# The relative bias of the second mixer: joined in SBUF by accumulating transfers, or by additions on GpSimd

## The chip, the cores and the metric

The kernel runs on one core of one Trainium2 chip. The metric is device time in microseconds (us), taken over whole executions; the time before is the median of three runs. Engines carry the names of the profile: PE is TensorE, PEld its weight load, DVE VectorE, ACT ScalarE, POOL GpSimd, SP SyncE.

## The reference

Two blocks of two layers each run over 256 tokens of 1024 channels. The first block has latent attention, a squared-relu MLP, block attention with a relative bias, and another MLP; the second has a gated delta rule and a forgetting attention. The change concerns the bias of the block attention. With 256 tokens there is one block, so nothing is selected, and what is left is causal attention with eight heads of 128 channels:

```python
def rel_bias(pq, pk):
    return table_h[h_i4, t5_bucket(pq - pk)].astype(jnp.float32)
...
lg_own = (jnp.einsum('bhqd,bhtd->bhqt', qi, k_own).astype(jnp.float32) * scale
          + rel_bias(pq4, pos_own[:, None, None, :]))
causal = (own * MOBA_BLOCK + t_ids)[None, :] <= q_idx[:, None]
parts.append(jnp.where(causal, lg_own, -jnp.inf))
```

`t5_bucket` turns the distance of a query and a key into one of 32 buckets, and `table_h` has a number for each head and bucket.

## The kernel before

All matrix products of weights are made of three products of rounded parts. `load_w` (L148) brings 512 KB of weights into one of four buffers `raw` over SyncE's queue (L161), ScalarE rounds them to `whi` (L164), VectorE, or GpSimd where the call says so, subtracts to get `wlo` (L165), and `mm3` issues the products (L171 to L173). A buffer `raw` is free for the next load when its `wlo` is done. The instructions are written in one program order, layer by layer; a planner puts them on the engines' queues by when their inputs should be there, so an instruction may stand far ahead of its place in the program if it waits for nothing. Each engine then takes its queue strictly in order.

The bias is made during the first MLP, which runs 16 steps `f` of 256 hidden channels. Each step loads two pieces of `mlp_w_in` and two of `mlp_w_out`. `rel_bias_step` (L379) hangs on each step: VectorE makes masks that say which keys each bucket reaches (L377), TensorE multiplies them by the differences of the table (L393), and ScalarE copies the result to a staging buffer (L395), of which there are two. The table is in two parts, a rounded one and the rest, so there are two partial sums, `part` 0 and 1. After every second step `b`, eight transfers of 64 KB on GpSimd's queue send the staging buffer to `bias_d` in DRAM (L400); `bias_d` is [part, query, head, key].

After the MLP `rel_bias_finish` (L403) reads it back so that queries lie on partitions. Two transfers bring part 0 into `bias` (L404, L405), four bring part 1 into two buffers `b2` (L409, L410), and for each half of the heads GpSimd adds the two parts (L411) and the causal mask (L412): four additions of 128 x 1536 numbers. `bias` is [128, 8 heads, 384]: the first 128 columns are the first 128 queries against the first 128 keys, the other 256 the second 128 queries against all keys. It lies in `bias_s`, beside the positions `pk` and `pq` from which the masks are made. `attend` (L312) adds it to the logits, first at L321.

The second mixer `moba` (L720) follows. It transposes x (L256, L257, L271), takes the mean square and its inverse root (`ms_eps`, `rsqrt` with L182 to L187, VectorE's work on 128 x 2 numbers), and projects queries, keys and values (`qkv_quad`, L682) before the first head is attended to.

The program at its end is `mla()`, `rel_bias_setup()`, `mlp(0, ...)` with the bias step, `rel_bias_finish()`, `moba()`, `mlp(1)`, `gdn()`, `fox()`. `rel_bias_setup` makes `pk`, `pq` and the table's differences, and clears their tile `tw` (L367).

Of the kernel before, what the change touches and what calls it, by code (L numbers as in the profile page):

```python
# [19 lines left out]
P = 128  # L20
# [4 lines left out]
H = 8  # L25
# [17 lines left out]
# smallest distance of each of the 32 relative-position buckets; the first takes every distance below 1  # L43
# [15 lines left out]
def layout(inputs):  # L59
    """The small operands side by side as [128, n]: constants, gains with one channel on each  # L60
    partition, rows that every partition needs; and where each begins and ends."""
# [10 lines left out]
    # causal mask for [query tile 0 x keys 0..127 | query tile 1 x keys 0..255]  # L72
# [23 lines left out]
    # identity columns of the 32 x 32 blocks that the partitions (column half, block, unit) solve for  # L96
# [14 lines left out]
def kernel(ctx: ExitStack, tc: tile.TileContext, I: dict, out: bass.AP, small_at: dict):  # L111
# [11 lines left out]
    # ------------------------------------------------------------------ helpers  # L123
    def slot(i, shape, dt=F32):
        """one of the 8 KB (8: 16 KB) places that the stages share"""
        return big.tile(shape, dt, tag=f"s{i}", name=f"s{i}")
# [13 lines left out]
    @contextmanager  # L140
    def queued(after):
        """what the block issues comes behind the instructions given, each on its engine"""
        with ExitStack() as es:
            for i in after or ():
                es.enter_context(tc.issue_after(i))
            yield

    def load_w(src, a, b, engines=None, into=None, after=None):  # L148
        """DRAM [128, a, b] -> for each i < a the two float32r parts, [128, b] each"""
        m = max(1, 1024 // b)  # L150
        parts = []
        for a0 in range(0, a, m):
            k = min(m, a - a0)
            raw = ring.tile([P, 1024], F32, tag="raw", name="raw")
            if into is None:
                hi = ring.tile([P, 1024], F32R, tag="whi", name="whi")
                lo = ring.tile([P, 1024], F32R, tag="wlo", name="wlo")
            else:
                hi, lo = (t[:, a0 * b:(a0 + k) * b] for t in into)
            rs = raw[:, :k * b]  # L160
            nc.sync.dma_start(rs.rearrange("p (a b) -> p a b", a=k), src[:, a0:a0 + k])  # L161
            e = V if engines is None else engines[a0 // m % len(engines)]
            with queued(after):
                A.activation(hi[:, :k * b], rs, AF.Copy)  # L164
                e.tensor_tensor(lo[:, :k * b], rs, hi[:, :k * b].bitcast(F32), op=ALU.subtract)  # L165
            for i in range(k):
                parts.append((hi[:, i * b:(i + 1) * b], lo[:, i * b:(i + 1) * b]))
        return parts
# [9 lines left out]
    def rsqrt(dst, x, n):  # L178
        """dst = x ** -0.5 for [128, n] tiles"""
# [9 lines left out]
    def rsqrt_sum(r, e, a, b):  # L189
        """r = ((a + b) / D + eps) ** -0.5 for [128, 1] tiles; e [128, 2] is room; D = 4 ** 5"""  # L190
# [9 lines left out]
    # ------------------------------------------------------------------ inputs and constants  # L200
# [18 lines left out]
    # keep the tensor engine's clock up until the first weights are here  # L219
# [4 lines left out]
    # per-channel scales that carry the attention scale too  # L224
# [7 lines left out]
    # ------------------------------------------------------------------ shared stages  # L232
    def mean_sq(dst, src_t, t):
        """dst [128, 2]: sums of squares of the two halves of a token tile"""
        for hf in range(2):
            j = w2k([P, 512])
            A.activation(j, src_t[:, t, hf * 512:(hf + 1) * 512], AF.Square, accum_out=dst[:, t, hf:hf + 1])

    def ms_eps(src, name, after=None):
        """[128, 2]: mean square over the row, plus eps"""  # L240
# [9 lines left out]
    def evac_split(hi, lo, p, g=None):  # L250
        """PSUM p (times a per-partition gain) into two float32r parts"""
# [11 lines left out]
    def transpose_x(src, gnames, slots):  # L263
        """src token-major [128, 2, 1024] -> for each gain the split transposed [128, 8, 256]"""
# [17 lines left out]
    def proj_tok(hT, w, c0, n):  # L282
        """token-major product of hT (1024 rows) and columns c0..c0+n (n <= 512): two accumulators"""
# [10 lines left out]
    def out_proj(oT, w, then, between=None):  # L294
        """oT [128, 8, 256] times w [1024, 1024] by column halves; then(t, half, psum)"""
# [16 lines left out]
    def attend(logits, scale, bias, v, oT, h):  # L312
        """one head: logits(ps) fills [128, 384]; scale: None or [128, 1] per query tile; v [128, 2, 128]"""
# [36 lines left out]
    # ------------------------------------------------------------------ relative bias for the second mixer  # L350
    bias = bias_s[:, 0:3072].rearrange("p (h k) -> p h k", h=H)
    bias_d = dr.tile([2, S, H, S], F32, tag="bias_d", name="bias_d")

# [20 lines left out]
    def masks(i, pq, pk):  # L374
        """which keys each of the 32 buckets reaches, for four groups of queries"""
# [3 lines left out]
    def rel_bias_step(i, pq, pk, tw):  # L379
        """four of the 64 groups; every eighth group sends what there is to DRAM"""  # L380
# [15 lines left out]
        if half == 1:  # L396
            for part in range(2):
                for q4 in range(4):
                    r0 = part * 32 + q4 * 8
                    nc.gpsimd.dma_start(  # L400
                        bias_d[part, 64 * q4 + 8 * b:64 * q4 + 8 * b + 8].rearrange("g h k -> h g k"), stg[r0:r0 + 8])

    def rel_bias_finish():  # L403
        nc.gpsimd.dma_start(bias[:, :, 0:128], bias_d[0, 0:128, :, 0:128])  # L404
        nc.gpsimd.dma_start(bias[:, :, 128:384], bias_d[0, 128:256])  # L405
        for h4 in range(2):
            hs = slice(4 * h4, 4 * h4 + 4)
            b2 = slot(13 + h4, [P, 4, 384])
            nc.gpsimd.dma_start(b2[:, :, 0:128], bias_d[1, 0:128, hs, 0:128])  # L409
            nc.gpsimd.dma_start(b2[:, :, 128:384], bias_d[1, 128:256, hs])  # L410
            G.tensor_tensor(bias[:, hs], bias[:, hs], b2, op=ALU.add)  # L411
            G.tensor_tensor(bias[:, hs], bias[:, hs], cmask[:, None, :].to_broadcast([P, 4, 384]), op=ALU.add)  # L412

    # ------------------------------------------------------------------ layer 0: latent attention
    def rope_tables():
# [7 lines left out]
        # quarter turn for the cosine enters with the turn count, so that the reduction stays exact  # L423
# [29 lines left out]
    def rope_apply(eng, dst, src, tab, nh):  # L453
        """src, dst [128, 2, nh, 64]; tab: the cosine and the sine table with the gain in them"""
# [8 lines left out]
    def mla():  # L463
# [65 lines left out]
        # eps terms of the per-head norms: the rows still carry the scale of the norms before  # L529
# [84 lines left out]
    # ------------------------------------------------------------------ squared-relu MLP  # L614
    def mlp(l, extra=None):
# [16 lines left out]
        for f in range(NF):  # L632
            wc = load_w(w1[:, :, f * 256:(f + 1) * 256], KD, 256, (G,) if f == 0 else None, after=last if f == 1 else None)
            r = w2k([P, 512])
            if f == 0:
                # the upper half of the rows comes last out of the stage before
# [38 lines left out]
    # ------------------------------------------------------------------ layer 1: block attention with relative bias  # L675
    def head_sumsq(dst, src):
        """dst [128, 4]: sums of squares of four heads of src [128, 512]"""
# [4 lines left out]
    def qkv_quad(hTq, hTk, wq, cq, wkk, ck, wv, cv, es, g4, gq, gk, qT, kT, vt, vscale, a=None):  # L682
        """four heads: q transposed (its norm is left to the logits: rq), k normed and transposed, v"""
# [57 lines left out]
    # ------------------------------------------------------------------ norms of the second block  # L741
    def row_scale(r, rb):
        """r [128, 2] with the tokens along the free axis, on every partition"""
# [5 lines left out]
    def post_norm_out(oT, w, gname, after, between=None):  # L749
        """x += rms_norm(oT.T @ w) * gain; after(t) once a token tile is done"""  # L750
# [20 lines left out]
    def softplus_neg(dst, u_in, n):  # L771
        """dst = log(1 + exp(-u_in)) for u_in >= 0, by the series of the inverse hyperbolic tangent"""
# [18 lines left out]
    # ------------------------------------------------------------------ gated delta rule  # L791
    def gdn():
# [7 lines left out]
        # gates  # L800
# [30 lines left out]
        # running sums of the log decays in each chunk, as columns and as rows  # L831
# [30 lines left out]
        def conv(part, dst, hp):  # L862
            """two heads: product, causal depthwise convolution over time, silu; channels on partitions"""
# [20 lines left out]
        def token_sumsq(dst, p, hp):  # L884
            """sums of squares of two heads of tokens, p [128, (t, head, channel)]"""
# [6 lines left out]
        # keys: their products within a chunk, and the diagonal blocks of the triangular system  # L892
# [32 lines left out]
        # inverses of the 32 x 32 diagonal blocks: partition (half of the columns, block, unit)  # L925
# [12 lines left out]
        def substitute(j):  # L938
            """row j of the inverse is done: take its part out of the rows below"""
# [59 lines left out]
        def gate(q4):  # L999
            """the gate of four heads, with the gain of the output norm in it"""  # L1000
# [6 lines left out]
        def grow_a(s, u4):  # L1007
            """block inverses from s to 2 s; X[:, 0] the inverse, X[:, 1] its transpose"""
# [46 lines left out]
        # chunk 0, the state it leaves, chunk 1  # L1055
# [28 lines left out]
        def solve(t, q4):  # L1084
            """what the chunk adds to the state, on the scale of the keys as they are"""
# [48 lines left out]
    # ------------------------------------------------------------------ forgetting attention  # L1134
    def fox():
# [3 lines left out]
        # the first token tile goes ahead while the second one is still being normed  # L1139
# [64 lines left out]
        def gates():  # L1204
            # the row scale along the free axis
# [31 lines left out]
    # ------------------------------------------------------------------ program  # L1237
    mla()
    rb = rel_bias_setup()
    mlp(0, lambda f: rel_bias_step(f, *rb))  # L1240
    rel_bias_finish()
# [28 lines left out]
```

## Time and profile before

| | us |
|---|---|
| median of three runs | 1002.09 |
| lowest, highest run | 1000.29, 1003.99 |
| span of the profiled execution | 996.2 |

The profile gives the profiled execution's time as its span, from the first to the last instruction; it has no other time for it, and the runs' times, taken around a whole execution, are some 6 us longer. Times in a row count from the span's start. A row of a timeline has the start, the duration, the engine, the line, the operation, what it writes and reads, and in brackets how long the engine had been idle and what ended that. [...]

### The profile page before, as it was taken

Reading aid. Unit: us, or ns where it says so; the run is one execution under the profiler, and the core shown is the slowest. Engines: PE = TensorE matmul, PEld = TensorE weight load, DVE = VectorE, ACT = ScalarE, POOL = GpSimd, SP = SyncE. Lnnn points to the kernel's source line nnn. Section 1 sums busy time; section 2 is a strip of 40 time slices with the busy share of each in tenths; the row PEclk is TensorE's granted clock in tenths of the full one; section 3 lists DMA queues with packets and bytes.
Section 4 is the critical chain, followed back from the end, with each engine's and each line's share of the span. In section 5 each row is a group of like instructions: output and inputs, shape, how many; then the busy total and the mean of one; then the engine's idle time right before and its main releaser. Section 6 shows DMA issues by size and latency. Waiting matters only on the chain.

```text
span 996.2 us, 14682 instructions
## 1 busy us (share of the span) xinstructions
PE 913.5 (92%) x5462; PEld 792.4 (80%) x5462; DVE 673.7 (68%) x1323; ACT 516.1 (52%) x954; POOL 202.5 (20%) x217
## 2 busy tenths in 40 slices
PE   9699889999999889999999999878879897999996
PEld 8576579999997677778999999668877785789874
DVE  6897476556555875766545554669996588767766
ACT  7574354645454545656544444357634224856653
POOL 1320121111122700022000002243496403000000
PEclk9899799999999989999999999979999999999998
DMA  8343237666667555435665666334646204365431
GB/s 294 104 148 106 64 117 230 203 191 191 193 196 242 173 169 166 141 110 191 207 206 174 188 197 180 93 86 127 159 128 179 76 22 132 103 217 184 132 123 64
DMA packets 96552, 154.61 MB, mean 155 GB/s; under 512 B 9160, under 2 KB 60128, under 8 KB 96224
## 3 DMA queue, kind: packets, MB, share of 16 engines
q1 hardware_dynamic: 91168, 141.53, 45.9%
q0 software_dynamic: 5168, 12.10, 4.4%
q8 instruction: 43, 0.70, 0.3%
q14 instruction: 29, 0.24, 0.1%
q10 hardware_dynamic: 144, 0.03, 0.0%
HBM read 147.84 MB, written 5.78 MB: 154 GB/s over the span
## 4 chain that ended last, share of the span: by engine, by line
PE 51%; DVE 17%; DMA 13%; ACT 8%; issue 5%; POOL 5%; SPq 0%; DVEq 0%; ACTq 0%; POOLq 0%
PE acc L171 11%; PE acc L172 10%; PE acc L173 10%; DMA raw<-in_mlp_w_in_dram 7%; DVE wlo L165 4%; ACT whi L164 3%; PE aux L173 3%; PE aux L171 3%; PE aux L172 3%; POOL s L943 2%; POOL s L941 2%; DVE s L165 2%; DVE rs_b L185 1%; PE aux L1026 1%; PE aux L335 1%
## 5 line engine op out<-in xcount | busy, mean ns | idle before, releaser
L165 DVE TENSOR_TENSOR wlo<-raw,whi 128x1024 fp32r<-128x1024 f32 (+2 forms) x182 | 225.5, 1244 | 185.1 <-ACT whi L164 172.7
L164 ACT ACTIVATE whi<-raw 128x1024 fp32r<-128x1024 f32 (+3 forms) x206 | 210.6, 1025 | 228.3 <-DMA raw<-in_mlp_w_in_dram 131.9
L172 PE MATMUL acc<-wlo,s 128*128 128x512 f32 (+2 forms) x424 | 167.6, 396 | 8.6 <-DVE wlo L165 8.3
L171 PE MATMUL acc<-whi,s 128*128 128x512 f32 (+2 forms) x424 | 169.8, 405 | 4.6 <-ACT whi L164 2.9
L173 PE MATMUL acc<-whi,s 128*128 128x512 f32 (+2 forms) x424 | 166.5, 396 | 0.0
L173 PE MATMUL aux<-s,wlo 128*128 128x256 f32 (+2 forms) x528 | 150.2, 284 | 3.0 <-DVE wlo L165 3.0
L171 PE MATMUL aux<-s,whi 128*128 128x256 f32 (+2 forms) x528 | 150.2, 285 | 2.1 <-DVE s L257 2.1
L172 PE MATMUL aux<-s,whi 128*128 128x256 f32 (+2 forms) x528 | 149.9, 284 | 0.0
L165 POOL TENSOR_TENSOR wlo<-raw,whi 128x1024 fp32r<-128x1024 f32 (+2 forms) x24 | 55.2, 2316 | 241.3 <-ACT whi L164 240.5
L171 PEld LDWEIGHTS aux<-s,whi 128*128 128x128 f32 (+2 forms) x528 | 99.8, 189 | 4.6 <-DVE s L257 2.6
L173 PEld LDWEIGHTS aux<-s,wlo 128*128 128x128 f32 (+2 forms) x528 | 99.8, 189 | 4.4 <-DVE wlo L165 3.4
L171 PE MATMUL acc<-s,w2k 128*128 128x512 f32 x256 | 100.1, 391 | 2.4 <-ACT w2k L656 2.4
L172 PEld LDWEIGHTS acc<-wlo,s 128*128 128x128 f32 x424 | 81.9, 193 | 24.8 <-DVE wlo L165 11.2
L172 PEld LDWEIGHTS aux<-s,whi 128*128 128x128 f32 (+2 forms) x528 | 99.9, 189 | 1.9
L171 PEld LDWEIGHTS acc<-whi,s 128*128 128x128 f32 x424 | 81.1, 192 | 24.9 <-ACT whi L164 4.4
L173 PE MATMUL acc<-s,w2k 128*128 128x512 f32 x256 | 100.2, 392 | 0.1
L172 PE MATMUL acc<-s,w2k 128*128 128x512 f32 x256 | 100.1, 391 | 0.0
L173 PEld LDWEIGHTS acc<-whi,s 128*128 128x128 f32 x424 | 81.5, 192 | 15.5 <-DVE s L254 0.6
L165 DVE TENSOR_TENSOR s<-raw,s 128x1024 fp32r<-128x1024 f32 x60 | 70.8, 1220 | 4.8 <-ACT s L164 4.8
L172 PE MATMUL acc<-s,whi 128*128 128x256 f32 x256 | 73.6, 288 | 0.0
L171 PE MATMUL acc<-s,whi 128*128 128x256 f32 x256 | 73.5, 287 | 0.0
L173 PE MATMUL acc<-s,wlo 128*128 128x256 f32 x256 | 73.4, 287 | 0.0
(351 smaller groups left out, 1569.8 us busy)
## 6 DMA issues: line engine op xcount, KB each, us to landing
raw<-in_mlp_w_in_dram SPq DMA_DIRECT2D x64, 512.0 KB, 5.0
raw<-in_mlp_w_out_dram SPq DMA_DIRECT2D x64, 512.0 KB, 3.9
raw<-in_gdn_w_in_dram SPq DMA_DIRECT2D x32, 512.0 KB, 4.0
raw<-in_moba_w_qkv_dram SPq DMA_DIRECT2D x24, 512.0 KB, 4.1
raw<-in_fox_w_in_dram SPq DMA_DIRECT2D x16, 512.0 KB, 4.8
raw<-in_kv_w_dram SPq DMA_DIRECT2D x16, 512.0 KB, 4.0
raw<-in_mla_w_o_dram SPq DMA_DIRECT2D x8, 512.0 KB, 3.9
bias_d<-s POOLq DMA_DIRECT2D x64, 64.0 KB, 4.3
```

Source lines behind the costliest of these rows:

```text
L164: A.activation(hi[:, :k * b], rs, AF.Copy)
L165: e.tensor_tensor(lo[:, :k * b], rs, hi[:, :k * b].bitcast(F32), op=ALU.subtract)
L171: T.matmul(o, lhsT=l[0], rhs=r[0], start=start, stop=False)
L172: T.matmul(o, lhsT=l[0], rhs=r[1], start=False, stop=False)
L173: T.matmul(o, lhsT=l[1], rhs=r[0], start=False, stop=stop)
L185: V.scalar_tensor_tensor(b, dst, -0.5, x, op0=ALU.mult, op1=ALU.mult)
L335: T.transpose(pt[:, j * P:(j + 1) * P], pr[:, j * P:(j + 1) * P], ident)
L941: G.tensor_tensor(t3[:, 0:n, 0:c], xb[:, j, 0:c][:, None, :].to_broadcast([P, n, c]), bt[:, j, j + 1:32][:, :, None].to_broadcast([P, n, c ...
L943: G.tensor_tensor(xb[:, j + 1:32, 0:c], xb[:, j + 1:32, 0:c], t3[:, 0:n, 0:c], op=ALU.subtract)
L1026: T.matmul(px[z][:, j * P:(j + 1) * P], lhsT=a, rhs=b, start=True, stop=True)
```

## The change

Before the first MLP a new function writes the causal mask into `bias`, once for each head, by one transfer from the input `small` in DRAM on GpSimd's queue. `rel_bias_finish` goes, with its six loads, its buffers `b2` and its four additions. In its place a gather follows every second set of stores (after b = 1, 3, 5 and 7): for both parts and four groups of 64 queries, a transfer of 16 queries from `bias_d` that adds to what lies in `bias`. A transfer writes 16 partitions, 8 heads and 128 or 256 columns. The rest of the diff takes out comments and texts of functions, which changes no instruction.

```diff
+    def rel_bias_mask():
+
+        nc.gpsimd.dma_start(bias, I["small"][:, None, small_at["cmask"][0]:small_at["cmask"][1]].to_broadcast([P, H, 384]))
...
                     nc.gpsimd.dma_start(
                         bias_d[part, 64 * q4 + 8 * b:64 * q4 + 8 * b + 8].rearrange("g h k -> h g k"), stg[r0:r0 + 8])
-
-    def rel_bias_finish():
-        nc.gpsimd.dma_start(bias[:, :, 0:128], bias_d[0, 0:128, :, 0:128])
-        nc.gpsimd.dma_start(bias[:, :, 128:384], bias_d[0, 128:256])
-        for h4 in range(2):
-            hs = slice(4 * h4, 4 * h4 + 4)
-            b2 = slot(13 + h4, [P, 4, 384])
-            nc.gpsimd.dma_start(b2[:, :, 0:128], bias_d[1, 0:128, hs, 0:128])
-            nc.gpsimd.dma_start(b2[:, :, 128:384], bias_d[1, 128:256, hs])
-            G.tensor_tensor(bias[:, hs], bias[:, hs], b2, op=ALU.add)
-            G.tensor_tensor(bias[:, hs], bias[:, hs], cmask[:, None, :].to_broadcast([P, 4, 384]), op=ALU.add)
-
+            if b % 2:
+                rel_bias_gather(b - 1)
+
+    def rel_bias_gather(b):
+
+        for part in range(2):
+            for q4 in range(4):
+                p0, r = 64 * (q4 % 2) + 8 * b, 64 * q4 + 8 * b
+                a0, n = ((0, 128), (128, 256))[q4 // 2]
+                nc.gpsimd.dma_start(bias[p0:p0 + 16, :, a0:a0 + n], bias_d[part, r:r + 16, :, 0:n], accum_op=ALU.add)
...
     mla()
+    rel_bias_mask()
     rb = rel_bias_setup()
     mlp(0, lambda f: rel_bias_step(f, *rb))
-    rel_bias_finish()
     moba()
```

## Rows read from the trace of the kernel before

**Rows 1.** The page, busy time, share and instructions of each engine.

```profile
PE 913.5 (92%) x5462; PEld 792.4 (80%) x5462; DVE 673.7 (68%) x1323; ACT 516.1 (52%) x954; POOL 202.5 (20%) x217
```

**Rows 2.** Waits from 320 to 352 us: in total, times, longest.

```profile
PE acc L172 <- DVE wlo L165: 7.6, 1, 7.6
...
POOL s L411 <- DMA s<-bias_d: 5.6, 1, 5.6
```

**Rows 3.** Chain of waits, 318 to 352 us: start, duration, what.

```profile
334.69 4.47 DVE wlo L165
...
350.31 1.15 DVE wlo L165
```

**Rows 4.** Timeline of GpSimd: the first and the last of four additions.

```profile
334.58 3.50 POOL L411 TENSOR_TENSOR s<-s,s 128x1536 f32<-128x1536 f32 x1 [5.59 <-DMA s<-bias_d]
...
346.01 3.42 POOL L412 TENSOR_TENSOR s<-s,small 128x1536 f32<-128x1536 f32 x1
```

**Rows 5.** Timeline of VectorE in the same stretch.

```profile
333.40 1.23 DVE L165 TENSOR_TENSOR wlo<-raw,whi 128x1024 fp32r<-128x1024 f32 x1
...
346.19 3.27 DVE L185 SCALAR_TENSOR_TENSOR rs_b<-r,mse 128x2 f32<-128x2 f32 x1
349.49 0.16 DVE L186 TENSOR_TENSOR rs_b<-rs_b,r 128x2 f32<-128x2 f32 x1
```

**Rows 6.** Timeline of TensorE around its gap.

```profile
343.52 0.39 PE L171 MATMUL acc<-whi,s 128*128 128x512 f32 x1
351.50 0.80 PE L172 MATMUL acc<-wlo,s 128*128 128x512 f32 x1 [7.59 <-DVE wlo L165]
...
355.42 0.39 PE L172 MATMUL acc<-wlo,s 128*128 128x512 f32 x1
```

**Rows 7.** Windows: length, then busy (count) by engine, clock, DMA share, GB/s.

```profile
351.50:355.40 3.90, 3.90 (x9) 3.11 (x10) 3.90 (x4) 0.00 (x0) 0.00 (x0) 0.51 0.71 201
```

**Rows 8.** Timeline of ScalarE: the rounding behind the late `wlo`.

```profile
338.78 1.05 ACT L164 ACTIVATE whi<-raw 128x1024 fp32r<-128x1024 f32 x1
```

**Rows 9.** Timeline of GpSimd at the start.

```profile
0.88 0.20 POOL L367 MEMSET tw<- 128x128 f32 x1
```

**Rows 10.** Windows: the first loads, and the quiet stretch before the first MLP.

```profile
4.00:20.00 16.00, 14.74 (x84) 13.82 (x83) 12.17 (x40) 12.79 (x23) 1.83 (x2) 1.00 0.98 350
...
120.00:135.00 15.00, 12.91 (x69) 10.66 (x69) 8.27 (x19) 5.90 (x15) 0.00 (x0) 0.89 0.00 1
```

**Rows 11.** Chain of waits, 0 to 26 us.

```profile
9.25 7.96 DMA x<-in_x_dram
```

**Rows 12.** The page, DMA queues: packets, MB, share of 16 engines.

```profile
q0 software_dynamic: 5168, 12.10, 4.4%
```

**Rows 13.** Chain of waits, 150 to 560 us: loads inside the first MLP.

```profile
204.62 6.57 DMA raw<-in_mlp_w_in_dram
...
217.76 4.62 DMA raw<-in_mlp_w_in_dram
...
228.93 5.52 DMA raw<-in_mlp_w_in_dram
...
289.69 4.68 DMA raw<-in_mlp_w_in_dram
...
300.92 6.16 DMA raw<-in_moba_w_qkv_dram
```

**Rows 14.** Timeline of GpSimd: two of the eight sets of stores.

```profile
225.26 4.44 POOL L400 DMA_DIRECT2D bias_d<-s  x8 [19.88 <-ACT s L395]
248.53 4.44 POOL L400 DMA_DIRECT2D bias_d<-s  x8 [18.83 <-ACT s L395]
```

**Rows 15.** Instructions on `bias_d`: issue in ns, first and last start; landing.

```profile
L400 POOL DMA_DIRECT2D bias_d<-s x64: 562/562/842, 151.3 to 322.3; - x64
...
DMA to landing us min/median/max: 3.0/4.4/8.5
```

**Rows 16.** Instructions of line 321, `attend`: ns, first and last start.

```profile
L321 DVE SCALAR_TENSOR_TENSOR w2k<-aux,r,s x32: 341/412/480, 379.3 to 978.1; 128x128 f32<-128x128 f32 x16, 128x256 f32<-128x256 f32 x16
```

## The prediction

> **What bounds the kernel now.** The page comes first. TensorE is busy 92% of the span [rows 1], so an edit on GpSimd or on the DMA queues gains only where TensorE stands still, and costs only where it makes TensorE stand. I then read the waits around the edited code, between the first MLP and the second mixer. There the longest wait of TensorE is 7.6 us for a `wlo` of VectorE [rows 2]. The chain of waits passes the same place: from 334.69 to 350.31 it runs over VectorE alone, and its first step is a `wlo` of 4.47 us [rows 3]. The reader is to see that this is no long work: the same `wlo` took 1.23 us just before, and a 128x2 step that takes 0.16 us a little later takes 3.27 us here [rows 5]. What else was going on is in GpSimd's timeline: four additions of 128x1536, back to back, from 334.58 to 349.43 [rows 4]. The stretched steps of VectorE end where these end. So I read it as one engine keeping the other out: VectorE does four stretched steps in the time of four additions, and the `wlo` that TensorE needs waits behind them.
>
> TensorE's timeline gives the price. A matmul starts at 343.52, the next at 351.50, and the usual pace is back at 355.42 [rows 6]. The gap is about 7.75 us. [...] In all **9.6 us**.
>
> **The change part by part.**
>
> *Four additions leave GpSimd.* VectorE is then free from 334.6. The `whi` that the waiting `wlo` needs is started at 338.78 and takes 1.05 us [rows 8], so with 1.23 us the `wlo` is ready at about 341.1, before TensorE wants it at 343.75. I take the whole **-9.6 us**; the bounds are -7.75 (the gap alone, if the clock drops at some other pause) and -9.6. Late next are later weight loads, which this stage refills four at a time and which also start earlier once VectorE frees their buffers, so nothing takes the gap's place.
>
> *Six loads of 3.1 MB at 324 to 334 go.* Eight smaller transfers of 0.79 MB, the last gather, take their place. GpSimd alone waited for those loads, and I give 0 for it, either way: TensorE's wait in that stretch is for VectorE [rows 2].
>
> *The mask transfer is added.* It writes 128 x 8 x 384 x 4 bytes = 1.57 MB into SBUF. In the program it stands behind the first mixer, but it waits for nothing, and an instruction of GpSimd's that stands just behind it in the program, the clearing of `tw`, runs at 0.88 us [rows 9]. So I expect the transfer at about 1 us, in the middle of the first loads. From 4 to 20 us the DMA engines are full: share 0.98, 350 GB/s [rows 10]. The chain of waits there goes through the load of `x`, 7.96 us long [rows 11]. Another 1.57 MB at 350 GB/s is 4.5 us of transfers that were not there, and `x` lands that much later. I take **+4.5 us**. The lower bound is 0, if the transfer runs in the quiet stretch from 120 to 135 us, DMA share 0.00 [rows 10]. The upper bound goes by the software queue's own pace: 4.4% of 996.2 us for 12.10 MB is 3.6 us per MB [rows 12], so 5.7 us.
>
> *Four gathers are added, three inside the first MLP.* A gather has two passes of four transfers, 0.39 MB each, 0.79 MB in all, so the four together move the 3.1 MB that the six loads moved. Here the chain of waits runs round a loop: load of `mlp_w_in`, `whi`, `wlo`, the next load [rows 13]. This load has no slack, so what delays it delays the end. A set of stores (0.52 MB) already shows what such traffic costs. The five loads that follow a set directly took 6.2 us on the mean (6.57 first, 6.16 last), the four between them 4.68 (4.62 first, 4.68 last) [rows 13]. That is 1.5 us for 0.52 MB, or 2.9 us per MB. The first pass of a gather starts when the set behind it has been issued and landed, at 229.7 for the set of 225.26 with 4.44 us of issues [rows 14]. So it meets the loads of `mlp_w_in` in flight from 228.93: 0.39 x 2.9 = 1.1 us. The second pass falls on the loads of `mlp_w_out`, whose data is used a whole step later, and costs nothing as long as it is over before the next load of `mlp_w_in`, 11 to 13 us after the one before (204.62 to 217.76, 217.76 to 228.93) [rows 13]. Three gathers make **+3.4 us**; the fourth meets the stretch that the six loads leave. No row shows an accumulating transfer. The lower bound is 0 (all of it falls beside `mlp_w_out`). The upper bound lets both passes count (2.3 us) and doubles that, because adding reads the old value too: 4.6 us each, 13.7 in all. I take the plain price because the nearest rows, the stores, are of the same queue, size and loop.
>
> [...]
>
> *Waits on GpSimd's queue.* A gather waits for its stores, and its second pass waits for the first to land, because both add to the same bytes. Behind it on the queue are only the next stores, which come at 248.53 after 18.83 us of idle [rows 14]. With issues of 0.56 us and a landing of 4.4 us [rows 15] the gather is through its issues at about 229.7 + 2.3 + 4.4 + 2.3 = 239, so the stores are not held up. If the eight transfers were held apart one by one it would be 229.7 + 8 x 5 = 270, the stores would be late, and ScalarE would wait for their buffer. For the last gather the one who waits is the first use of the bias, at 379.3 [rows 16], about 370 after the gain. The last set is issued at 322.3, so the gather is complete by about 341, or 353 with the longest landing of 8.5 us [rows 15] in its three places: covered, at no cost.
>
> **Sum.** -9.6 + 4.5 + 3.4 = -1.7 us on the span of 996.2 us. The profile gives no time beside the span; the median of the runs, 1002.1, is 5.9 us above it, and I carry that over: **1000.4 us**.
>
> **The rivals.**
> - *The mask is hidden.* It runs in the quiet stretch, or the first loads have room for it. For: I have shown a place in the program, not a place in time, and the quiet stretch is there. Against: the clearing of `tw` ran at 0.88 us, and the DMA share is full from 4 to 20 us. -9.6 + 3.4 = -6.2, or 995.9 us.
> - *The gathers are hidden.* They fall beside `mlp_w_out` altogether. -9.6 + 4.5 = -5.1, or 997.0 us; with the mask hidden too, 992.5.
> - *Accumulating is dear, and the time gets longer.* The place is the load of `mlp_w_in` after stores 1, 3 and 5. For: the loop has no slack, and adding needs the old value. Against: half of a gather falls where slack is. At the upper bound -9.6 + 4.5 + 13.7 = +8.6, or 1010.7 us. It ends slower by over 0.5% from (5.0 + 5.1) / 3 = 3.4 us per gather, three times my price.
> - *The change doesn't do what it says.* VectorE's stretched steps have another cause than the additions, and the gap stays: +7.9, or 1010.0 us. Against: four additions and four stretched steps lie over each other.
>
> **How the numbers follow.** The forecast has 0.43, the hidden mask 0.20, the hidden gathers 0.14, dear accumulation 0.19, no effect 0.04. A measurement of this kernel can tell about 0.5%, or 5.0 us, from no change. Faster by more than that are the hidden mask (0.20), just over half of the hidden gathers (0.08) and 0.07 of the forecast where its costs are at the lower ends: 0.35. Slower are most of dear accumulation (0.17) and the last case with part of its neighbours (0.03): 0.20. The rest is 0.45. The forecast's own range is 996 to 1005. The range runs from both hidden, 992.5, to 1009.5, close under dear accumulation's full price.
>
> **What would show it.** Right: no TensorE gap near 344 us and a `wlo` of 1.2 us throughout; the mask transfer on GpSimd at about 1 us, and the load of `x` landing 4 us or so later; loads of `mlp_w_in` near 6 to 7 us three times more. Wrong: the mask issued after 100 us; loads of 9 us and more after a gather; stores that wait behind a gather; TensorE waiting for the bias at the first head.

## The result, and the profile after

The changed kernel takes **1033.1 us**, the median of four runs (1031.9 to 1035.3), against 1001.2 for the kernel before in the same comparison: ratio 1.0327, 95% interval 1.0302 to 1.0352. It is 32 us slower, outside the range, and on the side that the forecast thought least likely.

The profiled execution of after has a span of 1033.5 us and took 1035.3 us, so only 1.8 us lie outside the span. The span of 996.2 us before therefore belongs, if as little lies outside it, to an execution of some 998 us, a quick one, and not to one of 1002; the two spans lie 37.3 us apart where the medians lie 31.9 apart. Read stages from the spans, prices from the medians.

The windows show where the time went. They are cut at the first transposition of the MLP (L271), the first update of x behind it (L673 before, L676 after), and the last update of x by the second mixer (L310). Columns are length, busy time (count) by engine, granted clock (TensorE's, as a share of its full speed), DMA share, GB/s. First the kernel before, then after:

```profile
0.00:129.70 129.70, 110.62 (x525) 86.14 (x526) 91.60 (x273) 72.56 (x201) 26.87 (x33) 0.93 0.43 137
129.70:323.30 193.60, 188.83 (x1225) 171.67 (x1224) 117.36 (x165) 103.37 (x147) 41.59 (x66) 1.00 0.65 201
323.30:445.70 122.40, 113.86 (x547) 90.23 (x547) 85.98 (x159) 64.42 (x118) 26.00 (x14) 0.97 0.49 150
445.70:996.20 550.50, 500.15 (x3170) 444.38 (x3168) 378.79 (x727) 275.72 (x488) 107.99 (x105) 0.97 0.48 144
```

```profile
0.00:130.40 130.40, 112.11 (x525) 87.66 (x526) 88.49 (x273) 72.53 (x201) 28.04 (x34) 0.92 0.45 149
130.40:345.80 215.40, 197.13 (x1226) 176.69 (x1225) 117.95 (x166) 104.85 (x147) 61.76 (x88) 0.95 0.70 191
345.80:479.60 133.80, 118.38 (x547) 94.09 (x546) 75.10 (x159) 64.50 (x118) 15.23 (x15) 0.96 0.46 128
479.60:1033.50 553.90, 499.82 (x3170) 444.00 (x3168) 378.87 (x728) 276.24 (x488) 110.83 (x104) 0.97 0.46 142
```

The start costs 0.7 us more, the first MLP 21.8, the second mixer 11.4, the rest 3.4. TensorE does the same work in each stage, so I put its extra busy time (8.3 us in the MLP) down to the lower granted clock (0.95 there, where before had 1.00), and what is left of the 21.8 us is standing still.

Three things are as forecast. The mask's transfer went to the very start of GpSimd's queue, and the clearing of `tw` that had stood at 0.88 us [rows 9] now stands behind it (GpSimd's timeline):

```profile
1.32 1.06 POOL L356 DMA_DIRECT2D s<-in_small_dram  x1 [0.38 <-issue]
2.37 0.23 POOL L371 MEMSET tw<- 128x128 f32 x1
```

VectorE's stretched steps are gone. The step of 128x2 that took 3.27 us and the `wlo` of 4.47 us [rows 3, 5] have their plain lengths, in VectorE's timeline at the same place of the program, and TensorE has no gap there:

```profile
357.38 1.22 DVE L165 TENSOR_TENSOR wlo<-raw,whi 128x1024 fp32r<-128x1024 f32 x1
...
359.09 0.16 DVE L185 SCALAR_TENSOR_TENSOR rs_b<-r,mse 128x2 f32<-128x2 f32 x1
359.28 0.16 DVE L186 TENSOR_TENSOR rs_b<-rs_b,r 128x2 f32<-128x2 f32 x1
```

And no store stands behind a gather: in GpSimd's timeline a set of stores still waits for ScalarE's copies alone, as in [rows 14]. The gather follows in two passes:

```profile
230.60 4.46 POOL L404 DMA_DIRECT2D bias_d<-s  x8 [18.68 <-ACT s L399]
235.05 3.71 POOL L415 DMA_DIRECT2D s<-bias_d  x4
244.07 3.42 POOL L415 DMA_DIRECT2D s<-bias_d  x4 [5.31 <-DMA s<-bias_d]
```

Two things are not. In the chain of waits, the loads of `mlp_w_in` that follow a gather take 8.4 and 10.5 us, where [rows 13] had 4.6 to 6.6:

```profile
185.75 10.47 DMA raw<-in_mlp_w_in_dram
199.73 4.79 DMA raw<-in_mlp_w_in_dram
211.07 5.78 DMA raw<-in_mlp_w_in_dram
223.43 4.29 DMA raw<-in_mlp_w_in_dram
235.42 8.35 DMA raw<-in_mlp_w_in_dram
```

And the order of the instructions is another one. Compared by source line and tiles in the two traces, at least 139 of TensorE's matmuls, 41 of ScalarE's instructions and 29 of VectorE's stand at another place in their queues. In the MLP, from step 8 on, the copies to the staging buffer come late and two steps at a time: ScalarE's timeline has four at 263.96, where each step had its two (229.25).

```profile
229.25 1.06 ACT L399 ACTIVATE s<-aux 64x512 f32<-64x512 f32 x2
...
254.48 1.06 ACT L164 ACTIVATE whi<-raw 128x1024 fp32r<-128x1024 f32 x1 [7.22 <-DMA raw<-in_mlp_w_in_dram]
255.44 0.58 ACT L654 ACTIVATE w2k<-aux 128x512 f32<-128x512 f32 x1
...
263.96 2.02 ACT L399 ACTIVATE s<-aux 64x512 f32<-64x512 f32 x4
```

TensorE pays at once. Its bias matmuls (L397) now need a PSUM buffer that a relu of ScalarE (L654) frees, and that relu stands behind a rounding that waits for a load. The bias matmul stands ahead of weight products on TensorE's queue, so they wait too (timeline of TensorE, the longest gap of the MLP):

```profile
256.08 0.69 PE L397 MATMUL aux<-s,tw 128*64 128x256 f32 x2 [8.13 <-ACT w2k L654]
```

In the second mixer the first head's logits (L346) are there at 388.1, but the first addition of the bias (L321) runs at 411.6, 23.5 us later; before it was 7.2 us (372.1 and 379.3). VectorE's timeline shows that it waits for nothing there: it is simply placed behind the `wlo` of the next four heads' weights. The last gather had been issued at 354.8.

```profile
410.48 1.23 DVE L165 TENSOR_TENSOR wlo<-raw,whi 128x1024 fp32r<-128x1024 f32 x1 [2.85 <-ACT whi L164]
411.62 0.34 DVE L321 SCALAR_TENSOR_TENSOR w2k<-aux,r,s 128x128 f32<-128x128 f32 x1
```

My reading of what follows is that once the heads begin, few projections are left to fill TensorE between their softmax steps. From the x update to the mixer's end TensorE has 13 gaps of over 0.5 us, 14.65 us together; the longest is this one:

```profile
448.13 0.41 PE L709 MATMUL aux<-gains,s 128*128 128x128 f32 x2 [4.54 <-DVE s L702]
```

So there were two theories. **Late loads:** the gathers, narrow and adding, hold up the loads of `mlp_w_in`. **The order:** the planner takes the gathers for long, and where it puts the staging copies and the first head costs more than the transfers do.

### The profile page after: what moved, and what is told of

The parts are those of the page before. It is cut to its first block, busy times and chain, and to the rows that moved or that the text cites. A ratio compares the mean times of both kernels' runs of the same rounds, so it can differ in the third digit from the quotient of the medians.

```text
span 1033.5 us, 14722 instructions
## 1 busy us (share of the span) xinstructions
PE 927.4 (90%) x5462; PEld 802.4 (78%) x5462; DVE 660.4 (64%) x1323; ACT 518.1 (50%) x954; POOL 215.9 (21%) x240
## 3 DMA queue, kind: packets, MB, share of 16 engines
q0 software_dynamic: 9280, 13.67, 6.6%
## 4 chain that ended last, share of the span: by engine, by line
PE 55%; DVE 13%; DMA 12%; ACT 7%; issue 6%; POOL 5%; SPq 0%; DVEq 0%; ACTq 0%; POOLq 0%
PE acc L171 12%; PE acc L172 12%; PE acc L173 12%; DMA raw<-in_mlp_w_in_dram 10%; PE aux L171 3%; PE aux L172 3%; PE aux L173 3%; ACT whi L164 3%; POOL s L944 2%; POOL s L946 2%; DVE wlo L165 2%; DVE s L165 2%; PE aux L1029 1%; PE aux L335 1%; PE aux L608 1%
## 5 line engine op out<-in xcount | busy, mean ns | idle before, releaser
L165 DVE TENSOR_TENSOR wlo<-raw,whi 128x1024 fp32r<-128x1024 f32 (+2 forms) x182 | 222.9, 1228 | 202.4 <-ACT whi L164 200.9
L164 ACT ACTIVATE whi<-raw 128x1024 fp32r<-128x1024 f32 (+3 forms) x206 | 210.9, 1027 | 236.8 <-DMA raw<-in_mlp_w_in_dram 133.4
L171 PEld LDWEIGHTS acc<-whi,s 128*128 128x128 f32 x424 | 82.1, 195 | 28.4 <-ACT whi L164 6.5
L171 PE MATMUL acc<-s,w2k 128*128 128x512 f32 x256 | 102.2, 399 | 1.5 <-ACT w2k L659 1.5
L173 PE MATMUL acc<-s,w2k 128*128 128x512 f32 x256 | 102.2, 399 | 1.0 <-DVE w2k L660 0.9
L172 PE MATMUL acc<-s,w2k 128*128 128x512 f32 x256 | 102.1, 399 | 0.0
L172 PEld LDWEIGHTS acc<-wlo,s 128*128 128x128 f32 x424 | 82.5, 195 | 16.8 <-DVE wlo L165 3.6
L173 PEld LDWEIGHTS acc<-whi,s 128*128 128x128 f32 x424 | 82.6, 195 | 15.9 <-DVE s L1231 0.5
L164 ACT ACTIVATE s<-raw 128x1024 fp32r<-128x1024 f32 x64 | 64.3, 1049 | 20.5 <-PE acc L173 13.5
```

The costliest lines, as they stand in the source:

```text
L171: T.matmul(o, lhsT=l[0], rhs=r[0], start=start, stop=False)
L172: T.matmul(o, lhsT=l[0], rhs=r[1], start=False, stop=False)
L173: T.matmul(o, lhsT=l[1], rhs=r[0], start=False, stop=stop)
```

## The experiments

Diffs are against the kernel after unless another is named. "MLP" and "mixer" are the lengths of those two windows in the run's own profile: 193.6 and 122.4 us before, 215.4 and 133.8 after.

**1. The same gathers without adding.** A plain transfer overwrites, so the mask and part 0 are lost from the bias. TensorE, VectorE, ScalarE and SyncE have the order of after.

```diff
-                nc.gpsimd.dma_start(bias[p0:p0 + 16, :, a0:a0 + n], bias_d[part, r:r + 16, :, 0:n], accum_op=ALU.add)
+                nc.gpsimd.dma_start(bias[p0:p0 + 16, :, a0:a0 + n], bias_d[part, r:r + 16, :, 0:n])
```

> The changed kernel with the gathers as plain copies (the sums and the mask are overwritten, so the bias is that of part 1 alone); the order of instructions on TensorE, ScalarE, VectorE and SyncE is that of the changed kernel. Theory A (adding in a transfer holds the DMA engines so long that the loads of mlp_w_in come late): the first load after a gather falls from 10.5 us to about 6 to 7, the software queue's share from 6.6% to about 5%, and the time from 1033 to 1015 to 1022 us. Theory B (the planner, which takes the gathers to be long, has put ScalarE's copies and the first head late): the same order gives 1029 to 1034 us.

1036.2 us, ratio 1.0339 (1.0321 to 1.0357): no faster than with adding. That adding does have a price shows on GpSimd and in the queue's share of the DMA engines (5.4% here, 6.6% after). The instructions of L415, issue in ns min/median/max and first and last start, plain and then after:

```profile
L415 POOL DMA_DIRECT2D s<-bias_d x32: 528/530/620, 182.7 to 351.9; - x32
```

```profile
L415 POOL DMA_DIRECT2D s<-bias_d x32: 830/1122/1881, 182.9 to 354.8; - x32
```

The software queue in the page's list of DMA queues (packets, MB, share), plain and then after:

```profile
q0 software_dynamic: 5952, 13.67, 5.4%
```

```profile
q0 software_dynamic: 9280, 13.67, 6.6%
```

An issue takes twice as long and the same bytes hold the engines 22% longer, but none of it is on the path. "Accumulating is dear" falls as a mechanism: the loads behind a plain gather are as late (8.77 and 10.09 us).

**2. Four staging buffers in place of two**, so that the copies need not wait for the stores.

```diff
-            rel["stg"] = slot(9 + b % 2, [64, 8, S])
+            rel["stg"] = slot((9, 10, 13, 14)[b % 4], [64, 8, S])
```

> The changed kernel with four staging buffers in place of two; inside the first MLP the order on TensorE is then that of the kernel before, while the gathers move the same bytes. Theory A: the loads of mlp_w_in are as late as in the changed kernel, 1028 to 1033 us. Theory B: the gap of 8.1 us at 256 and those of 2.5 us at 284 and 322 go; the MLP ends 8 to 14 us earlier, 1019 to 1025 us; the first head still starts late.

1029.9 us, ratio 1.0273 (1.0254 to 1.0291). TensorE's order in the MLP is that of before again, the gap of 8.13 us is gone, and the MLP falls from 215.4 to 203.2 us. The loads after the three gathers stay late (9.16, 8.41, 8.69 us). But the mixer grows to 140.6 us: its first logits are there at 375.3, and the first addition of the bias stands at 411.6 us, to a tenth where it stood in after, though the x update came 9.6 us sooner (336.2 and 345.8). More than half of what the MLP gains the mixer gives back. VectorE's timeline and the window of the mixer:

```profile
411.61 0.34 DVE L321 SCALAR_TENSOR_TENSOR w2k<-aux,r,s 128x128 f32<-128x128 f32 x1
```

```profile
336.20:476.80 140.60, 121.57 (x547) 96.60 (x546) 75.67 (x159) 65.41 (x118) 14.14 (x13) 0.93 0.45 121
```

**3. The mask alone, no gathers** (the relative bias is left out).

```diff
-            if b % 2:
-                rel_bias_gather(b - 1)
```

> The changed kernel without the gathers: the bias is the mask alone. Theory A and B alike: all of the loss is with the gathers, 990 to 996 us, with the mask transfer at about 1 us costing what is left of 0.5 to 1 us at the start. Over 1005 us would put the loss on the mask or on moba.

995.1 us, ratio 0.9912 (0.9879 to 0.9945); MLP 195.8, mixer 113.8. So the whole loss hangs on the gathers: 38 us between this kernel and after. It also gives the plain price of the three loads that meet a gather in experiment 2 (chain of waits, the same loads of the MLP; the second and third follow a set of stores here too):

```profile
185.19 4.82 DMA raw<-in_mlp_w_in_dram
...
230.20 6.66 DMA raw<-in_mlp_w_in_dram
...
278.14 5.61 DMA raw<-in_mlp_w_in_dram
```

Against these, the gathers of experiment 2 delayed the loads by 4.3, 1.8 and 3.1 us, 3.1 us on the mean.

**4. The mask, and four whole-tile accumulating loads behind the MLP** in place of 32 narrow gathers.

```diff
-            if b % 2:
-                rel_bias_gather(b - 1)
+    def rel_bias_finish():
+        for part in range(2):
+            nc.gpsimd.dma_start(bias[:, :, 0:128], bias_d[part, 0:128, :, 0:128], accum_op=ALU.add)
+            nc.gpsimd.dma_start(bias[:, :, 128:384], bias_d[part, 128:256], accum_op=ALU.add)
...
     mlp(0, lambda f: rel_bias_step(f, *rb))
+    rel_bias_finish()
     moba()
```

> The mask as in the changed kernel, no gathers in the MLP, and after it four accumulating loads of whole tiles, two for each part; the order is nearly that of the kernel before. Both theories: no loss in the MLP, and TensorE's gap of 7.6 us near 344 us is gone. If the four loads land by 370 us, 991 to 995 us; if adding is three times as dear as a plain load the last lands at about 324 + 30 = 354, still covered. Above 1000 us would mean that the additions were not what held VectorE.

993.9 us, ratio 0.9917 (0.9888 to 0.9946), faster than both. TensorE's order differs from that of before in three matmuls, and the mixer's window shows what the additions had cost: 112.4 us at full clock, where before had 122.4 at 0.97.

```profile
130.80:327.50 196.70, 191.24 (x1225) 172.69 (x1224) 117.35 (x165) 103.10 (x147) 42.40 (x67) 0.99 0.64 198
327.50:439.90 112.40, 111.52 (x547) 89.11 (x547) 73.61 (x159) 64.50 (x118) 11.56 (x8) 1.00 0.63 162
```

Against after's mixer the 21.4 us are 6.9 us of TensorE's busy time and 14.5 us of standing still: here it has one gap of over 0.5 us in that stretch (0.61).

**5. The kernel before without its four additions.**

```diff
-            G.tensor_tensor(bias[:, hs], bias[:, hs], b2, op=ALU.add)
-            G.tensor_tensor(bias[:, hs], bias[:, hs], cmask[:, None, :].to_broadcast([P, 4, 384]), op=ALU.add)
```

> The kernel before, with the four bulk additions on GpSimd left out (part 1 of the relative bias and the mask are left out of the output). If they hold VectorE up and TensorE with it, as forecast: 991 to 994 us, VectorE's 2.4 to 3.4 us steps near 330 to 350 us gone. Rival, that VectorE's long steps were hidden: 1000 to 1002 us.

991.7 us, ratio 0.9900 (0.9875 to 0.9925); before was 1001.6 in that comparison. The additions cost 10.0 us; the forecast's first term, -9.6, is right, place and size. VectorE's timeline again has steps of 0.16 us where [rows 5] had 3.27. The order of the mixer is not quite that of before here (at least 43 of TensorE's matmuls stand elsewhere); experiment 4, with three, shows the same gain in the mixer.

**6. The 32 narrow gathers behind the MLP.** TensorE, VectorE and SyncE have the order of experiment 2; only the place of the gathers differs.

```diff
-            if b % 2:
-                rel_bias_gather(b - 1)
...
     mlp(0, lambda f: rel_bias_step(f, *rb))
+    for b in (0, 2, 4, 6):
+        rel_bias_gather(b)
     moba()
```

> The same 32 narrow accumulating gathers, all issued behind the MLP. The MLP's instructions then stand in the order of before and no gather runs beside its loads; in the second mixer TensorE, VectorE and ScalarE have the order that they have with four staging buffers. Theory of the order: x update near 327 us, but the first head (L321) again far behind its logits, and 133 to 140 us from the x update to the mixer's end where the kernel with four whole-tile loads has 112.4: 1015 to 1022 us. Rival, that the gathers cost only by running beside the MLP's loads: 994 to 997 us.

1020.5 us, ratio 1.0179 (1.0140 to 1.0218). MLP 196.6, first logits 368.8, first addition of the bias 405.1, mixer 139.2. The rival falls: with nothing beside the MLP's loads, 26.6 us are lost against the four whole-tile loads. And against experiment 2, which has the same order, the gathers beside the loads are worth 9.5 us net by the medians; the MLP's window alone is 6.6 us shorter here.

**7. The gathers aside:** they add onto two tiles that nobody reads.

```diff
+        for i, n in ((13, 128), (14, 256)):
+            aside.append(slot(i, [P, H, n]))
+            nc.gpsimd.dma_start(aside[-1], I["small"][:, None, small_at["cmask"][0]:small_at["cmask"][0] + n].to_broadcast([P, H, n]))
...
-                nc.gpsimd.dma_start(bias[p0:p0 + 16, :, a0:a0 + n], bias_d[part, r:r + 16, :, 0:n], accum_op=ALU.add)
+                nc.gpsimd.dma_start(aside[q4 // 2][p0:p0 + 16], bias_d[part, r:r + 16, :, 0:n], accum_op=ALU.add)
```

> The gathers add onto two tiles that nobody reads, and the bias stays the mask alone (the relative bias is left out of the output). MLP in the order of after, second mixer freed from the gathers. Theory of the order: x update near 346 us as in after, but the mixer takes 112 to 115 us in place of 133.8, so 1009 to 1016 us. Rival, late loads alone: the transfers are the same, so 1030 to 1035 us.

1012.1 us, ratio 1.0099 (1.0072 to 1.0126). MLP 210.9, in the order of after; mixer 117.0. The same transfers run at the same places of the MLP (with 1.57 MB more to fill the two tiles, issued at 35 and 122 us), and 21 us are gone. Of these 16.8 lie in the mixer, whose heads no longer depend on the gathers and are placed 1.1 us behind their logits (384.0 and 385.1). That the MLP, in the same order, is 4.5 us shorter too is not explained.

**8. Aside, with four staging buffers.**

```diff
-            rel["stg"] = slot(9 + b % 2, [64, 8, S])
+            rel["stg"] = slot((9, 10, 3, 4)[b % 4], [64, 8, S])
```

> As the gathers aside (the relative bias left out of the output), with four staging tiles in place of two, so that the MLP too stands in the order of before; what is left of the cost is the gathers' transfers beside the loads. Theory of order and late loads together: x update near 336 us, mixer 112 to 115 us, 1000 to 1006 us. If the order is the whole loss: 993 to 997 us. If late loads are the whole loss: over 1025 us.

1007.0 us, ratio 1.0055 (1.0030 to 1.0080), 1 us above what was expected; MLP 201.5, mixer 116.1. Both orders mended, 12 us are left against the mask alone, whose MLP has the same order on TensorE; by the profiles 5.7 of them lie in the MLP and 2.3 in the mixer, where 40 matmuls stand elsewhere.

**9. Experiment 6 with the first head pinned:** TensorE's work for the second four heads is queued behind the first head's transposes.

```diff
+            with queued(pins[0:1] if g4 else None):
                 r8 = qkv_quad(hT, hT, w, 512 * g4, w, D + 512 * g4, w, 2 * D + 512 * g4, es, g4,
...
+                pins.append(rel["pt"].ins)
```

> All 32 narrow gathers behind the MLP, as before, but TensorE's work for the second four heads is queued behind the first head's transposes, so that the first head is worked on as soon as its logits are there. Theory of the order: the sums have long landed when the heads want them, so the mixer takes about 112 to 118 us from the x update in place of 139.2: 993 to 1001 us. Rival, that the bias truly comes late: the first head waits on VectorE for the gathers until 400 us, and 1013 us or more.

1008.1 us, ratio 1.0066 (1.0040 to 1.0092), mixer 125.6: between the two, and both were wrong about one thing. The order was worth 12.4 us here, but with the order gone the data was late in earnest. So of the 26.6 us of experiment 6 not all is order. GpSimd needs from 324.6 to 366.5 us to issue 32 gathers, and VectorE waits for them twice; TensorE, which the pin keeps from other work, stands 10.79 us (timelines of VectorE and TensorE):

```profile
368.70 0.35 DVE L321 SCALAR_TENSOR_TENSOR w2k<-aux,r,s 128x128 f32<-128x128 f32 x1 [1.93 <-DMA s<-bias_d]
...
373.05 0.48 DVE L321 SCALAR_TENSOR_TENSOR w2k<-aux,r,s 128x256 f32<-128x256 f32 x1 [3.67 <-DMA s<-bias_d]
```

```profile
375.29 0.88 PE L335 MATMUL aux<-gains,w2k 128*128 128x128 f32 x3 [10.79 <-DVE w2k L331]
```

**10. The change itself, with both orders mended:** experiment 2 with the pin of experiment 9, whose order it has on TensorE, VectorE and SyncE.

```diff
+            with queued(pins[0:1] if g4 else None):
                 r8 = qkv_quad(hT, hT, w, 512 * g4, w, D + 512 * g4, w, 2 * D + 512 * g4, es, g4,
```

> The change with both orders mended (four staging tiles, and the second four heads queued behind the first head's transposes); TensorE, VectorE and SyncE have the order of the kernel with late gathers and the same pin, so only the place of the gathers differs. Late loads cost 9 to 13 us: 1003 to 1010 us, the mixer 112 to 118 us. If the gathers beside the loads cost nothing with the order mended: 994 to 999 us.

1011.9 us, ratio 1.0096 (1.0062 to 1.0130), 2 us above what was expected; mixer 120.1 in place of 140.6. This is the decisive pair: the gathers are where they were in experiment 2, their data is what the first head adds, and 18 us go by queueing alone. The mixer's window, and VectorE's timeline, where the bias is taken without a wait:

```profile
333.70:453.80 120.10, 113.26 (x547) 90.67 (x546) 75.32 (x160) 64.89 (x118) 14.21 (x13) 0.97 0.50 138
```

```profile
375.86 0.35 DVE L321 SCALAR_TENSOR_TENSOR w2k<-aux,r,s 128x128 f32<-128x128 f32 x1
```

5.0 us of its mixer I put down to the pin: TensorE stands that long for the first head's softmax.

**11. A wide transfer of the same bytes aside**, in place of the eight narrow ones, against experiment 8. It reads rows of `small` and not `bias_d`.

```diff
-        for part in range(2):
-            for q4 in range(4):
...
+        with queued([rel["st"]]):
+            nc.gpsimd.dma_start(aside[0], I["small"][:, None, c0:c0 + 192].to_broadcast([P, H, 192]), accum_op=ALU.add)
```

> In place of the 32 narrow gathers aside, one accumulating load on 128 partitions behind every second step, of the same bytes (0.79 MB each, from the mask's rows; the relative bias is left out of the output). If the narrow shape, or the number of transfers, makes the loads late: 994 to 999 us and x update near 327 us. If the bytes on the shared engines do: 1003 to 1010 us and x update near 333 us, as with narrow ones.

1000.2 us, ratio 0.9983 (0.9961 to 1.0006): 6.8 us below the narrow ones, 5.1 above the mask alone, so neither expectation. The loads beside the wide transfers take 8.86, 6.12 and 7.46 us, 1.8 us more on the mean than the same loads in experiment 3, where the narrow gathers of experiment 2 cost 3.1. Yet in the profiles the MLP is as long (201.3 us against 201.5), and 2.5 us of the difference lie in the mixer (113.6 against 116.1), where 40 matmuls stand elsewhere. So transfers of these bytes delay the loads in the wide shape too. Whether the narrow shape or the number of transfers adds to it is not settled: the loads suggest it, the MLP's length does not show it. How the 12 us divide stays open.

**12. Experiment 4 with the mask's transfer later,** behind GpSimd's last rotation of the first mixer. All other engines keep the order of experiment 4.

```diff
-        nc.gpsimd.dma_start(bias, I["small"][:, None, small_at["cmask"][0]:small_at["cmask"][1]].to_broadcast([P, H, 384]))
+        with queued([rel[True]]):
+            nc.gpsimd.dma_start(bias, I["small"][:, None, small_at["cmask"][0]:small_at["cmask"][1]].to_broadcast([P, H, 384]))
...
-        eng.tensor_tensor(dst, dst, t2, op=ALU.add)
+        rel[eng is G] = eng.tensor_tensor(dst, dst, t2, op=ALU.add).ins
```

> The four whole-tile accumulating loads behind the MLP, with the mask's transfer issued behind GpSimd's last rotation of the first mixer (near 83 us, where the DMA engines are at 0.2 to 0.35) in place of 1 us; every other engine has the same order. If the mask at the start costs what was forecast (4.5 us, or the 1 to 3 us that the profiles show): 989.5 to 993 us. If it is covered: 994 us, the same as with the mask at the start.

**990.8 us** (988.1 to 991.6), ratio 0.9888 (0.9857 to 0.9918), the lowest median of the study. The transfer is issued at 82.68 us, and the MLP starts at 129.6 us where it had started at 130.8. The medians put the mask at the start at 3.0 us, the profiles at 1.2; the two intervals overlap, so its size is not settled between these.

The medians, which come from four comparisons whose kernel before lay between 1000.6 and 1001.6 us, make a ladder from the best version to the kernel after, one step at a time:

| kernel | us | step |
|---|---|---|
| mask at 83 us, four whole-tile loads (12) | 990.8 | |
| mask at 1 us (4) | 993.9 | +3.0, the start |
| 32 narrow gathers behind the MLP (6) | 1020.5 | +26.6, the first head placed late and, behind that, the sums late (9) |
| the gathers beside the MLP's loads (2) | 1029.9 | +9.5, late loads |
| two staging buffers (after) | 1033.1 | +3.2, staging copies placed late |

## Why the prediction was wrong

**The additions, -9.6: right.** The kernel without them gains 10.0 us, and the place is the one named: the mixer falls from 122.4 to 113.2 us. Of the forecast's 9.6 us, 7.75 are TensorE's gap [rows 6]; the other 1.9, for a slower pace behind the gap, no run shows alone. What the trace of before shows there is nine matmuls in 3.90 us at a granted clock of 0.51 [rows 7], 0.43 us from one start to the next (352.09, 352.52), where from 355.42 on it is 0.23 (355.42, 355.65): 1.8 us more for the nine. The reading of one engine keeping the other out agrees with the rows: a VectorE step of 0.16 us takes 3.27 us beside additions of 3.4 us [rows 4, 5], and 0.16 us at this place once these are gone. Elsewhere in after the same line, L185, still takes 2.32 us (at 673.3), beside GpSimd's own `wlo` work of 4.67 us for two (from 673.2). How the one holds up the other, no run shows. But after itself shows none of this gain, because its first head no longer comes early enough to use it.

**The mask, +4.5: the right place, too dear.** It was issued at 1.32 us as forecast, and costs 1.2 us by the profiles and 3.0 by the medians, inside the bounds of 0 and 5.7. What failed is the step "`x` lands that much later": from issue to landing the load of `x` took 9.3 us in place of 8.0, and the four of the transposed input 8.4 in place of 5.2 (medians of the list of DMA issues). The chain of waits at the start of after no longer has the load of `x` but one of the transposed input (8.72 us, where before had 4.80), so I read it that the mask's 4.5 us of transfers were spread over loads that were not all on the path.

**The gathers, +3.4: mis-sized by two to three.** The term was 1.1 us for each of three loads. Experiment 2 against the ladder's row above it gives 9.5 us by the medians and 6.6 us in the MLP's windows, and its loads took 9.16, 8.41 and 8.69 us where the same ones without gathers take 4.82, 6.66 and 5.61 (experiment 3): 3.1 us each. I had priced the first pass by the stores' rows and let the second fall beside `mlp_w_out`. Both steps are too kind: the gather's delay comes on top of that of the stores before it, and per load it is nearly three times my price. The upper bound, 13.7 us, was nearer, by a reason that experiment 1 refutes: plain gathers delay as much as adding ones. Whether the narrow shape has a part in it is not settled: experiment 11 changes shape and number together.

**The step that failed: that the order stays.** The sum put prices on transfers and waits and kept every instruction where it stood. "Nothing takes the gap's place" and, of the first use of the bias, "covered, at no cost" both took the time 379.3 [rows 16], less the gain, for a fact of the kernel, when it was a product of the planner. The section on the kernel before says that the planner goes by when inputs should be there; the change makes the bias depend on 32 transfers in a row in place of six loads and four additions, and the staging buffers are read by stores with gathers among them on the same queue. The data was in fact there in time (experiment 10: no wait), but the first head was placed 23.5 us behind its logits. With the first head pinned 18.0 us go (experiment 10 against 2), with the dependence cut 16.8 us of the mixer (experiment 7); with the staging copies' 3.2 us that makes 21.2 of the 31.9 us lost, two thirds (1033.1 to 1011.9). I did not list it as a rival. Of my signs of being wrong one came, a load of over 9 us after a gather (10.47); TensorE did not wait for the bias at the first head, and none of the signs pointed at the order. That the planner's own estimate of these transfers is too long is inferred from where it puts their readers; the runs show the order and its price, not the estimate.

**The waits on GpSimd's queue: right in what they cost.** No store is held up by a gather. The last gather is through its issues 13.6 us after its stores began (342.0 to 355.6), as reckoned; the one of 230.60 takes 16.9 us in place of the 13.7 reckoned. Of the rivals, "accumulating is dear" had the sign and the place of a third of the loss, with the wrong cause; "the gathers are hidden" is refuted by 9.5 us; "the mask is hidden" was as near to the 1.2 to 3.0 us as the forecast's 4.5.

## What to carry to other kernels

Where a planner lays out the queues, a changed dependence is a changed order: ask for every reader of the moved data where the planner will put it if it takes the new transfers for slow, and compare the order of the two programs before pricing any transfer. Many small transfers in one chain on one queue can be dearer than their bytes: here four whole-tile accumulating loads at the end, issued from 326.6 to 341.0 us, did all that 32 gathers did (324.6 to 366.5 us in experiment 9), with the gain kept. And an instruction that comes late only because of its place shows no wait in the profile (L321 at 411.62 us in after, 23.5 us behind its logits); look for the distance between a producer and its first reader.

## What the runs showed of the hardware that I had not expected

Adding costs GpSimd more than the path: an issue of 0.83 to 1.9 us in place of 0.53, and for the same 13.67 MB a queue share of 6.6% of 1033.5 us (68 us of 16 engines) in place of 5.4% (56 us). A gather of 0.79 MB delayed a 512 KB load beside it by 3.1 us on the mean (experiment 2 against 3), and a single wide transfer of the same bytes by 1.8 (experiment 11); plain gathers had loads as late as adding ones (8.77 and 10.09 us against 10.47 and 8.35).
